# A two-layer DiT block on one core: a fixed order in the V phase of the expert FFN, 1/sqrt on VectorE, and rows held back into the next mixer

## Chip, core and metric

One core of one Trainium2 chip runs the whole kernel in a single launch. The metric is the time of one execution in device microseconds (us). Engines are named as the profile names them: PE (TensorE matmul), PEld (its weight load), DVE (VectorE), ACT (ScalarE), POOL (GpSimd), SP (SyncE, which issues most DMAs).

## The reference, cut to what matters

256 latent tokens (`x`) and 256 context tokens (`ctx`) of width D = 1024 pass through two layers. Layer 0 has an "even" mixer, layer 1 an "odd" one (differential attention; context enters it as keys and values only). Behind each mixer stands a PEER FFN: every token picks 16 of 16384 experts in each of 8 heads. In layer 1 only the latents need the FFN.

```python
def rms_norm(x, g):
    y = x * lax.rsqrt(jnp.mean(x * x, axis=-1, keepdims=True) + EPS)
    return y * g

def modulate(x, g, shift, scale):
    return rms_norm(x, g) * (1 + scale) + shift

def chunk(t):                       # in peer_ffn: 128 tokens
    q = (t @ w_q).reshape(PEER_CHUNK, PEER_HEADS, 2, PEER_KEY_HALF)
    ...
    idx = jnp.take_along_axis(cand_i..., best_j, axis=-1)
    g = jax.nn.softmax(best_s, axis=-1)
    a = jnp.einsum('td,thkd->thk', t, u[idx])
    w = jax.nn.gelu(a) * g
    return jnp.einsum('thk,thkd->td', w, v[idx])

# one layer
hl = modulate(xl, norm_mix_g[layer], sh_m, sc_m)      # and hc from xc
yl, yc = mixer(hl, hc)
xl = xl + g_m * yl
hl = modulate(xl, norm_ffn_g[layer], sh_f, sc_f)
xl = xl + g_f * peer_ffn(hl, w_q, sub_keys, u, v)
# xc likewise in layer 0; six shifts, scales and gates: silu(c) @ w_mod + b_mod
# the end: rms_norm(xl, final_norm_g)
```

## The kernel before

**The FFN, computed densely.** `ffn` (L782) does not gather experts for most tokens. `dense` (L632) runs two phases over all 16384 experts. The U phase computes gelu(h·uT) in 32 chunks of 512 experts. The V phase takes 64 chunks of 256 experts: it multiplies the activations `dy`/`dyl` by the table of gates `dg`, transposes the product on PE and multiplies it by the rows `dv` of V, adding into PSUM (`wide`, `bank`) over all chunks. In layer 0 three blocks of 128 tokens go this way (nt = 3: two of latents, one of context), in layer 1 two (nt = 2). The activations of 16 (layer 0) or 22 (layer 1) of the 64 V chunks stay in SBUF (`dy`); the others go to DRAM (`ad`) and come back as `dyl`.

**Precision.** Each fp32 operand is split in a high part (fp32r, made on ACT: `dvh`, `dwh`, `wh`) and the rest (made on DVE: `dvl`, `dwl`, `wl`), and each product takes three matmuls: high·high (L753), high·low with `dvl` (L754) and low·high (L755).

**One V chunk, as the program is written.** For chunk n: `load_v` (L701) issues from SP `dg` (L706), `dyl` (L710) and two tiles of `dv` (L714, 128 experts each); `v_prep` (L717) makes `dvh` (L724) and `dvl` (L725) of both tiles; `w_prep` (L741) multiplies `dyl` by `dg` (L746) and lets `w_split` (L730) transpose (L733) and split (L737, L738); `v_mm` (L757) multiplies. The loop calls `v_prep(c + 1)`, `load_v(c + 2)`, `w_prep(c + 1)`, `v_mm(c)`. The rings: `dg`, `dyl`, `dv`, `dvh` and `dvl` have 3 buffers, `dwh` and `dwl` 2.

**Who sets the order.** A scheduler with a timeline of its own orders the instructions on each engine when the program is built, so that an engine's order differs from the written one. `tc.issue_after(i)` around an instruction puts it behind `i` on its engine. At run time each engine goes through its list in order: an instruction that waits holds up all behind it.

**The second block of context tokens.** The fourth block of layer 0's FFN goes by row gathers, which run beside the dense phases. `gather` (L547) lets POOL issue an indirect DMA (L549) for one row per token (512 KB, 4 buffers `row`); 256 of them fetch rows of U (dot products on DVE, L564), 128 rows of V, each added on DVE into `gacc` (L576). `beside` (L939) feeds 5, 2 or 3 of these steps per chunk; the odd mixer feeds what is left, 6 per step, then all (L1048). Only when `gacc` is complete is it scaled by a gate and added to `x` (`add_ffn`, L579), and only then can that block be normalised for the odd mixer.

**The end of layer 0 and the odd mixer.** `fin` (L804) makes the gate of the latents' FFN by 8 transposes (L316) and copies (L317), adds the sum of the FFN to `x` (L583 `yadd`, L584 `xl`), and `finish` (L944) calls `norm_T` (L320) for the latents: sum of squares on ACT (L327), 1/sqrt, scaling by DVE (L332 `xn`), transposes on PE (L337), shift and scale (L342, L345 `hf`), split (L348, L349 `h`). The odd mixer projects the latents to q, k and v (weights `wt` split at L187, L188; matmuls L206 to L208; rotation L997 to L1001, with a multiplication on POOL), computes the modulations 3 and 4 of layer 1 (weights `wm`, matmuls L286), and then normalises the context into `oh`, whose tiles are the buffers `row`, and projects it to k and v.

**1/sqrt.** `rsqrt` (L250) starts from an integer estimate on DVE (L253) and makes three Newton steps of 4 operations each on POOL (L255 to L258), for both token blocks together in `norm_T`, where POOL also does the mean (L328), for one block in `rms_scale` (L260), which also makes the final norm's factor.

## Time and profile before

| what | value |
|---|---|
| runs of the kernel | 2888.35, 2892.41, 2897.49 us; median 2892.41 us |
| profiled execution | 2891.71 us, span in the profile 2889.9 us |
| mean granted PE clock of it | 0.965 |
| busy share of the span | PE 90%, PEld 74%, DVE 71%, ACT 45%, POOL 19% |
| data moved by DMA | 735.49 MB, 255 GB/s over the span |

The stages of the profiled execution lie, in us of its span, as follows: layer 0's mixer to about 465, its U phase about 523 to 1098, its V phase 1098 to 1665; the transition to 1697; the odd mixer's projection of latents to 1797, its context and attention to 1912; layer 1's routing and U phase about 2000 to 2438, its V phase 2440 to 2872; the final norm to 2890.

How to read it: a busy share is a mean over these stages. Where an engine waits, the row names the instruction or transfer that ended the wait. The granted clock is a share of full speed.

### The profile page before, as it was taken

The page shows a single profiled execution, that of the slowest core. Times are in us where ns is not written, and L with a number is a line of the kernel's source. Part 1 is how long each engine was busy: PE and PEld are TensorE (multiplying, and loading weights), DVE is VectorE, ACT ScalarE, POOL GpSimd, SP SyncE. Part 2 cuts the span into 40 slices and gives each one's busy share as a digit, 9 for nine tenths or more (in the row PEclk, how much of TensorE's full clock was granted, in tenths as well). Part 3 has the DMA queues.
Part 4 walks back from the last instruction along what each step waited for, and adds up shares of the span by engine and source line. Part 5 has one row for each costly group of instructions (what it writes and reads, how often), then busy time and mean ns, then how long its engine had stood idle before and what let it go on. Part 6 is the DMA issues. An engine that isn't in the chain of part 4 may idle for free.

```text
span 2889.9 us, 40187 instructions
## 1 busy us (share of the span) xinstructions
PE 2610.9 (90%) x14161; PEld 2134.2 (74%) x14161; DVE 2038.6 (71%) x3904; ACT 1310.6 (45%) x2226; POOL 562.0 (19%) x531
## 2 busy tenths in 40 slices
PE   6999984689999989999999969988999999998786
PEld 4776954567777767888888867868888887886665
DVE  3335699999988877887787874766998555554454
ACT  3334432358673433333333334544599743443332
POOL 0000003343433444433344430000000000000000
PEclk9999997899999999999999979999999999999999
DMA  6453466899999999999999856233778975566664
GB/s 246 132 204 86 160 243 206 278 353 345 354 374 354 358 360 351 351 351 351 338 340 358 316 184 231 91 107 127 238 223 266 313 251 180 180 205 214 201 220 140
DMA packets 354634, 735.49 MB, mean 255 GB/s; under 512 B 35312, under 2 KB 182016, under 8 KB 351872
## 3 DMA queue, kind: packets, MB, share of 16 engines
q1 hardware_dynamic: 299136, 531.56, 54.9%
q0 software_dynamic: 55296, 201.35, 19.5%
q8 instruction: 112, 1.84, 0.3%
q14 instruction: 90, 0.74, 0.1%
HBM read 664.13 MB, written 68.68 MB: 254 GB/s over the span
## 4 chain that ended last, share of the span: by engine, by line
PE 50%; issue 16%; DMA 15%; DVE 9%; POOL 6%; ACT 3%; SPq 1%; DVEq 0%; POOLq 0%; ACTq 0%
DMA dyl<-ad 7%; POOL row L549 5%; PE bank L754 4%; PE bank L755 4%; PE bank L207 4%; PE bank L206 4%; PE bank L753 4%; PE bank L208 4%; DMA du<-in_peer_uT 2%; PE bank L671 2%; PE bank L672 2%; PE wide L755 2%; PE wide L754 2%; PE wide L753 2%; PE bank L670 2%
## 5 line engine op out<-in xcount | busy, mean ns | idle before, releaser
L549 POOL DMA_INDIRECT row<-in_peer_u,gidx x256 | 346.7, 1354 | 530.2 <-DVE row L564 423.8
L724 ACT ACTIVATE dvh<-dv 128x1024 fp32r<-128x1024 f32 x256 | 269.4, 1059 | 393.6 <-DMA dv<-in_peer_v 193.6
L657 ACT ACTIVATE duh<-du 128x1024 fp32r<-128x1024 f32 x256 | 271.1, 1062 | 273.3 <-DMA du<-in_peer_uT 217.9
L659 DVE TENSOR_TENSOR dul<-du,duh 128x1024 fp32r<-128x1024 f32 x256 | 310.4, 1218 | 106.6 <-ACT duh L657 105.5
L725 DVE TENSOR_TENSOR dvl<-dv,dvh 128x1024 fp32r<-128x1024 f32 x256 | 309.2, 1222 | 93.0 <-ACT dvh L724 92.9
L564 DVE SCALAR_TENSOR_TENSOR row<-row,hc 128x1024 f32<-128x1024 f32 x256 | 307.3, 1216 | 22.0 <-DMA row<-in_peer_u,gidx 21.6
L754 PE MATMUL bank<-dvl,dwh 128*128 128x512 f32 x768 | 300.9, 392 | 0.5 <-DVE dvl L725 0.5
L755 PE MATMUL bank<-dvh,dwl 128*128 128x512 f32 x768 | 299.8, 392 | 0.0
L188 DVE TENSOR_TENSOR wl<-wt,wh 128x512 fp32r<-128x512 f32 x256 | 177.9, 700 | 157.9 <-ACT wh L187 155.5
L753 PE MATMUL bank<-dvh,dwh 128*128 128x512 f32 x768 | 265.6, 398 | 2.2 <-ACT dvh L724 1.7
L670 PE MATMUL bank<-duh,h 128*128 128x512 f32 x512 | 197.0, 411 | 65.2 <-ACT duh L657 65.1
L187 ACT ACTIVATE wh<-wt 128x512 fp32r<-128x512 f32 x256 | 160.8, 631 | 205.7 <-PE bank L207 98.9
L671 PE MATMUL bank<-dul,h 128*128 128x512 f32 x512 | 213.9, 418 | 11.9 <-DVE dul L659 11.7
L671 PE MATMUL wide<-dul,h 128*128 128x512 f32 x512 | 209.0, 408 | 10.9 <-DVE dul L659 10.9
L549 POOL DMA_INDIRECT row<-in_peer_v,gidx x128 | 170.5, 1332 | 243.7 <-DVE gacc L576 223.7
L670 PE MATMUL wide<-duh,h 128*128 128x512 f32 x512 | 207.0, 404 | 7.5 <-ACT duh L657 7.4
L206 PE MATMUL bank<-h,wh 128*128 128x256 f32 x704 | 206.0, 294 | 5.4 <-ACT hf L342 5.4
L672 PE MATMUL bank<-duh,h 128*128 128x512 f32 x512 | 208.1, 406 | 0.0
L208 PE MATMUL bank<-h,wl 128*128 128x256 f32 x704 | 204.0, 291 | 3.6 <-DVE wl L188 3.6
L207 PE MATMUL bank<-h,wh 128*128 128x256 f32 x704 | 204.5, 291 | 1.1 <-DVE h L349 1.1
L672 PE MATMUL wide<-duh,h 128*128 128x512 f32 x512 | 203.5, 397 | 0.0
L255 POOL TENSOR_TENSOR rs_t<-rstd 128x2 f32<-128x2 f32 (+1 forms) x27 | 7.4, 273 | 936.0 <-DVE rstd L253 934.7
(279 smaller groups left out, 5905.5 us busy)
## 6 DMA issues: line engine op xcount, KB each, us to landing
du<-in_peer_uT SPq DMA_DIRECT2D x256, 512.0 KB, 6.0
dv<-in_peer_v SPq DMA_DIRECT2D x256, 512.0 KB, 5.7
table<-gst SPq DMA_DIRECT2D x80, 512.0 KB, 7.0
wm<-in_w_mod SPq DMA_DIRECT2D x56, 512.0 KB, 6.9
wt<-in_peer_w_q SPq DMA_DIRECT2D x96, 256.0 KB, 3.3
dg<-table SPq DMA_DIRECT2D x64, 384.0 KB, 7.0
ad<-da SPq DMA_DIRECT2D x45, 512.0 KB, 5.4
dyl<-ad SPq DMA_DIRECT2D x90, 256.0 KB, 5.4
```

Of the source, the lines that this page charges most:

```text
L206: self.T.matmul(out, lhsT=a, rhs=b, start=k == 0 and m == 0, stop=False)
L207: self.T.matmul(out, lhsT=a, rhs=b2, start=False, stop=False)
L208: self.last = self.T.matmul(out, lhsT=a2, rhs=b, start=False, stop=k == KT - 1 and m == len(outs) - 1).ins
L549: self.G.indirect_dma_start(out=t, out_offset=None, in_=table, in_offset=bass.IndirectOffsetOnAxis(ap=idx[:, s:s + 1], axis=0))
L659: V.tensor_tensor(tl, t, th.bitcast(F32), ALU.subtract)
L670: T.matmul(b, lhsT=hi[:, k, :], rhs=uh[k], start=k == 0, stop=False)
L671: T.matmul(b, lhsT=hi[:, k, :], rhs=ul[k], start=False, stop=False)
L672: T.matmul(b, lhsT=lo[:, k, :], rhs=uh[k], start=False, stop=k == KT - 1)
L725: V.tensor_tensor(tl, v, th.bitcast(F32), ALU.subtract)
L753: T.matmul(b, lhsT=wh, rhs=v[0], start=first, stop=False)
L754: T.matmul(b, lhsT=wh, rhs=v[1], start=False, stop=False)
L755: T.matmul(b, lhsT=wl, rhs=v[0], start=False, stop=last)
```

## The change

1. **V phase.** For PE, ACT and DVE a helper `placed` puts each step behind the step written before it on the same engine. `v_prep` and `v_mm` are split in halves (one `dv` tile each), the multiplication by `dg` becomes `y_mul`, and the loop is written as shown. `dv` gets 6 - nt buffers: 3 in layer 0 as before, 4 in layer 1.
2. **1/sqrt.** All of it moves to VectorE: per block 3 + 6 small operations. `norm_T` calls it once per block through `rms_scale`.
3. **Gate of the FFN.** It is made when 5 chunks of the V phase are left (`near`), in both layers, into a `dy` buffer.
4. **Rows.** `beside` feeds none in the last two chunks of layer 0's V phase; what is left then is fed in the odd mixer, and put behind the last `xn` of the latents' norm (`normed`).
5. **Modulation 3 of layer 1.** Its first loads begin 8 chunks ahead of the end of layer 0's V phase, its first half is computed with 3 chunks left (`aside`), its second half in `finish`. The odd mixer keeps modulation 4.

```diff
-    def rsqrt(self, y, v, n):
-        G = self.G
-        t = self.small.tile([P, 16], F32, name="rs_t")
-        self.V.tensor_scalar(y.bitcast(I32), v.bitcast(I32), -0.5, 1597463007.0, op0=ALU.mult, op1=ALU.add)
+    def rsqrt(self, y, ss, n, width):
+        V = self.V
+        v, t = (self.small.tile([P, 16], F32, name=f"rs_{x}")[:, :n] for x in "vt")
+        V.tensor_scalar(v, ss, 1.0 / width, EPS, op0=ALU.mult, op1=ALU.add)
+        V.tensor_scalar(y.bitcast(I32), v.bitcast(I32), -0.5, 1597463007.0, op0=ALU.mult, op1=ALU.add)
+        V.tensor_scalar(v, v, -0.5, None, op0=ALU.mult)
         for _ in range(3):
-            G.tensor_tensor(t[:, :n], y, y, ALU.mult)
-            G.tensor_tensor(t[:, :n], t[:, :n], v, ALU.mult)
-            G.tensor_scalar(t[:, :n], t[:, :n], -0.5, 1.5, op0=ALU.mult, op1=ALU.add)
-            G.tensor_tensor(y, t[:, :n], y, ALU.mult)
+            if n == 1:
+                V.scalar_tensor_tensor(t, y, v, y, op0=ALU.mult, op1=ALU.mult)
...
+            V.scalar_tensor_tensor(y, t, 1.5, y, op0=ALU.add, op1=ALU.mult)
...
-        for i in range(2):
-            V.tensor_scalar(xn[i], self.x[2 * s + i], r[:, i:i + 1], None, op0=ALU.mult)
+            r = self.rms_scale(self.x[2 * s + i], xn[i])
+            self.normed = V.tensor_scalar(xn[i], self.x[2 * s + i], r, None, op0=ALU.mult).ins
...
-                    t = vp.tile([P, D], F32, name="dv", bufs=3)
+                    t = vp.tile([P, D], F32, name="dv", bufs=6 - nt)
...
+            def placed(engine):
+                return tc.issue_after(last[engine]) if engine in last else ExitStack()
...
             for c in range(NC):
-                v_prep(c + 1)
+                near(NC - c)
+                y_mul(c + 1)
+                v_prep(c + 1, 0)
                 load_v(c + 2)
+                v_mm(c, 0)
                 w_prep(c + 1)
-                v_mm(c)
+                v_prep(c + 1, 1)
+                v_mm(c, 1)
...
+            def near(n):
+                if n == 5:
+                    gate.append(self.gate(modT, 5, 1, "c", yp, "dy", keep))
+                aside(n, yp, keep)
...
-                feed(5 if c < 26 else 2 if c < NC // 2 else 3)
+                feed(5 if c < 26 else 2 if c < NC // 2 else 3 if c < NC // 2 + NC - 2 else 0)
...
+            if n == 8:
+                mods.append(self.mod_steps(1, 3, mod1, Tags([(yp, "dy", keep)] * 8), "c", keep, Tags([(yp, "dy", keep)] * 2)))
+            if n in (8, 3):
+                next(mods[0])
...
+            def late_rows(n, normed=self.normed):
+                with tc.issue_after(normed):
+                    feed(n)
...
-            if 3 + c < 5:
-                self.modulation(1, 3 + c, modT, wk, "y", 4)
+            if c == 1:
+                self.modulation(1, 4, modT, wk, "y", 4)
```

How the orders move, at the three places of which the prediction speaks. First DVE in the middle of layer 1's V phase; the numbers behind the names are those of tiles, and tiles of one chunk have near numbers (the two `dv` of a chunk stand 2 and 4 above its `dyl`, the next chunk's about 50 higher). Before:

```order
L746 TENSOR_TENSOR dyl_25381<-dyl_25381,dg_25379 128x512
L725 TENSOR_TENSOR dvl_25276<-dv_25235,dvh_25275 128x1024
L725 TENSOR_TENSOR dvl_25322<-dv_25283,dvh_25321 128x1024
L738 TENSOR_TENSOR dwl_25344<-bank_25338,dwh_25343 128x512
L746 TENSOR_TENSOR dyl_25431<-dyl_25431,dg_25429 128x512
L725 TENSOR_TENSOR dvl_25326<-dv_25285,dvh_25325 128x1024
L725 TENSOR_TENSOR dvl_25372<-dv_25333,dvh_25371 128x1024
```

And with the change:

```order
L745 TENSOR_TENSOR dwl_25414<-bank_25408,dwh_25413 128x512
L730 TENSOR_TENSOR dvl_25418<-dv_25344,dvh_25417 128x1024
L752 TENSOR_TENSOR dyl_25390<-dyl_25390,dg_25388 128x512
L730 TENSOR_TENSOR dvl_25448<-dv_25392,dvh_25447 128x1024
L745 TENSOR_TENSOR dwl_25477<-bank_25471,dwh_25476 128x512
L730 TENSOR_TENSOR dvl_25481<-dv_25394,dvh_25480 128x1024
L752 TENSOR_TENSOR dyl_25453<-dyl_25453,dg_25451 128x512
```

Before, the multiplication of a chunk's `dyl` stood ahead of the splits of `dv` that belong to the chunks three and two earlier (`dyl_25431` ahead of `dv_25285` and `dv_25333`); now it stands just ahead of the split of its own chunk (`dyl_25390` ahead of `dv_25392`).

SP in the same phase, before:

```order
L714 DMA dv_24733<-in_peer_v1 128x1024
L710 DMA dyl_24831<-ad1_17939 128x2x256
L714 DMA dv_24735<-in_peer_v1 128x1024
L706 DMA dg_24979<-table1_17938 128x2x256
L714 DMA dv_24783<-in_peer_v1 128x1024
L710 DMA dyl_24881<-ad1_17939 128x2x256
L714 DMA dv_24785<-in_peer_v1 128x1024
L706 DMA dg_25029<-table1_17938 128x2x256
```

And with the change:

```order
L708 DMA dyl_24890<-ad1_18001 128x2x256
L712 DMA dv_24844<-in_peer_v1 128x1024
L704 DMA dg_24938<-table1_18000 128x2x256
L712 DMA dv_24892<-in_peer_v1 128x1024
L708 DMA dyl_24940<-ad1_18001 128x2x256
L712 DMA dv_24894<-in_peer_v1 128x1024
L704 DMA dg_24988<-table1_18000 128x2x256
L712 DMA dv_24942<-in_peer_v1 128x1024
```

Each round still has two `dv`, one `dg` and one `dyl`; before, a `dyl` was asked for between the two `dv` of the chunk two ahead of its own; now between the two `dv` of the chunk just ahead of its own, and `dv` has one buffer more.

Second, DVE at the end of layer 0's V phase, before (the last `dvl`, then the sum of the FFN is added to `x`):

```order
L576 SCALAR_TENSOR_TENSOR gacc<-row,ijgc,gacc 128x1024 x7
L583 TENSOR_TENSOR yadd<-bank,gate 128x512
L576 SCALAR_TENSOR_TENSOR gacc<-row,ijgc,gacc 128x1024
L583 TENSOR_TENSOR yadd<-bank,gate 128x512
L584 TENSOR_TENSOR xl_9947<-xl_9947,yadd 128x512
L576 SCALAR_TENSOR_TENSOR gacc<-row,ijgc,gacc 128x1024
L584 TENSOR_TENSOR xl_9947<-xl_9947,yadd 128x512
L583 TENSOR_TENSOR yadd<-bank,gate 128x512
L576 SCALAR_TENSOR_TENSOR gacc<-row,ijgc,gacc 128x1024
L583 TENSOR_TENSOR yadd<-bank,gate 128x512
L584 TENSOR_TENSOR xl_9949<-xl_9949,yadd 128x512
```

And with the change:

```order
L730 TENSOR_TENSOR dvl<-dv,dvh 128x1024
L581 TENSOR_TENSOR yadd<-bank,gate 128x512 x2
L582 TENSOR_TENSOR xl_9983<-xl_9983,yadd 128x512 x2
L581 TENSOR_TENSOR yadd<-bank,gate 128x512 x2
L582 TENSOR_TENSOR xl_9985<-xl_9985,yadd 128x512
L254 TENSOR_SCALAR rs_v<-ss 128x1
L582 TENSOR_TENSOR xl_9985<-xl_9985,yadd 128x512
L255 TENSOR_SCALAR rstd<-rs_v 128x1
L581 TENSOR_TENSOR yctx<-wide,gate 128x512
L256 TENSOR_SCALAR rs_v<-rs_v 128x1
L581 TENSOR_TENSOR yctx<-wide,gate 128x512
L582 TENSOR_TENSOR xl_9981<-xl_9981,yctx 128x512
```

The rows (`gacc`) that stood between the additions are gone from there; the small operations of the 1/sqrt stand in their place, 18 up to the last `xn`, and no row does. Before, 8 rows stood between the first `yadd` and the last `xn`.

Third, DVE in the odd mixer around the context's norm, before (its `xn` early, among the first splits of weights):

```order
L188 TENSOR_TENSOR wl<-wt,wh 128x512
L332 TENSOR_SCALAR xn<-xl_9943,rstd 128x1024
L332 TENSOR_SCALAR xn<-xl_9945,rstd 128x1024
L188 TENSOR_TENSOR wl<-wt,wh 128x512 x2
L999 TENSOR_TENSOR ru<-bank,c_rope 128x256 x2
L1001 TENSOR_TENSOR oq<-oq,ru 128x256
L188 TENSOR_TENSOR wl<-wt,wh 128x512
L1001 TENSOR_TENSOR oq<-oq,ru 128x256
```

And with the change (the end of the latents' part):

```order
L574 SCALAR_TENSOR_TENSOR gacc<-row,ijgc,gacc 128x1024
L188 TENSOR_TENSOR wl<-wt,wh 128x512
L574 SCALAR_TENSOR_TENSOR gacc<-row,ijgc,gacc 128x1024
L188 TENSOR_TENSOR wl<-wt,wh 128x512
L574 SCALAR_TENSOR_TENSOR gacc<-row,ijgc,gacc 128x1024 x2
L188 TENSOR_TENSOR wl<-wt,wh 128x512 x3
L574 SCALAR_TENSOR_TENSOR gacc<-row,ijgc,gacc 128x1024 x8
L581 TENSOR_TENSOR gacc<-gacc,gate 128x512 x2
L582 TENSOR_TENSOR xl_9979<-xl_9979,gacc 128x512 x2
L254 TENSOR_SCALAR rs_v<-ss 128x1
L255 TENSOR_SCALAR rstd<-rs_v 128x1
```

Before, the context's `xn` came 26 instructions behind the latents' last `xn`, one row among them. Now 56 rows stand between these two, spread over the 48 `wl`, with eight of them last; the gate, the addition to `x`, the 1/sqrt and `xn` come behind those. On POOL 43 gathers stand among the 16 multiplications of the rotation, the last 10 behind all of these.

## Rows read from the trace of the kernel before

**Rows 1.** Windows: stretch, length, busy us (instructions) of each engine, granted clock, DMA share, GB/s.
```profile
1098.00:1666.00 568.00, 562.74 (x2647) 464.70 (x2648) 457.30 (x550) 184.11 (x259) 235.44 (x176) 0.99 0.96 346
1666.00:1697.00 31.00, 4.77 (x21) 3.40 (x19) 27.08 (x41) 7.61 (x17) 12.44 (x20) 0.58 0.46 144
1697.00:1797.00 100.00, 96.48 (x703) 82.72 (x703) 56.42 (x111) 45.44 (x79) 17.73 (x29) 0.98 0.69 237
...
2500.00:2560.00 60.00, 60.00 (x286) 49.63 (x285) 30.52 (x30) 26.88 (x31) 0.00 (x0) 1.00 0.56 177
...
2571.00:2872.00 301.00, 259.46 (x1177) 202.67 (x1176) 144.52 (x161) 106.69 (x123) 0.00 (x0) 1.00 0.64 204
```

**Rows 2.** Waits in 2580:2865: total us, times, longest.
```profile
DVE dyl L746 <- DMA dyl<-ad: 141.8, 37, 5.8
PEld wide L754 <- DVE dvl L725: 56.7, 36, 3.6
```

**Rows 3.** Timeline of layer 1's V phase: start, us, engine, [idle before].
```profile
2643.28 0.69 DVE L746 TENSOR_TENSOR dyl<-dyl,dg 128x512 f32<-128x512 f32 x1 [3.92 <-DMA dyl<-ad]
...
2643.89 2.35 DVE L725 TENSOR_TENSOR dvl<-dv,dvh 128x1024 fp32r<-128x1024 f32 x2
...
2645.16 0.19 PEld L754 LDWEIGHTS wide<-dvl,dwh 128*128 128x128 f32 x1 [1.67 <-DVE dvl L725]
...
2645.55 0.39 SPq L710 DMA_DIRECT2D dyl<-ad  x1
...
2650.66 0.69 DVE L746 TENSOR_TENSOR dyl<-dyl,dg 128x512 f32<-128x512 f32 x1 [3.83 <-DMA dyl<-ad]
```

**Rows 4.** Timeline behind layer 1's V phase: gate, addition, 1/sqrt, last scaling.
```profile
2872.05 1.09 ACT L317 ACTIVATE gate<-bank 128x512 f32<-128x512 f32 x2 [7.59 <-PE bank L316]
2872.68 1.29 DVE L583 TENSOR_TENSOR yadd<-wide,gate 128x512 f32<-128x512 f32 x2 [6.96 <-ACT gate L317]
...
2877.77 0.19 POOL L255 TENSOR_TENSOR rs_t<-rstd 128x1 f32<-128x1 f32 x1 [929.23 <-DVE rstd L253]
...
2879.09 0.15 DVE L253 TENSOR_SCALAR rstd<-ms 128x1 int32<-128x1 int32 x1
...
2883.63 1.28 DVE L965 SCALAR_TENSOR_TENSOR fy<-xl,rstd,fg 128x1024 f32<-128x1024 f32 x1 [1.18 <-POOL rstd L258]
```

**Rows 5.** Timeline from the end of layer 0's V phase to the latents' first projection.
```profile
1657.10 1.86 POOL L549 DMA_INDIRECT row<-in_peer_v,gidx  x1 [1.78 <-DVE gacc L576]
...
1665.20 0.91 PEld L316 LDWEIGHTS bank<-c_ident,modT 128*128 128x128 f32 x7
...
1680.34 0.96 POOL L549 DMA_INDIRECT row<-in_peer_v,gidx  x1 [0.50 <-DVE yctx L583]
...
1682.07 1.16 POOL L255 TENSOR_TENSOR rs_t<-rstd 128x2 f32<-128x2 f32 x1 [0.77 <-DVE rstd L253]
...
1686.10 0.20 POOL L255 TENSOR_TENSOR rs_t<-rstd 128x2 f32<-128x2 f32 x1
...
1688.27 1.42 DVE L332 TENSOR_SCALAR xn<-xl,rstd 128x1024 f32<-128x1024 f32 x2 [2.57 <-POOL rstd L258]
...
1697.09 0.58 PE L207 MATMUL bank<-h,wh 128*128 128x256 f32 x1 [1.07 <-DVE h L349]
```

**Rows 6.** Timeline: the context's first projection.
```profile
1797.13 0.39 PE L206 MATMUL bank<-oh,wh 128*128 128x256 f32 x1 [1.54 <-ACT hf L342]
```

**Rows 7.** Groups by line, DVE in 1666:1797, then PE in 1697:1797: busy us, mean ns.
```profile
L188 DVE TENSOR_TENSOR wl<-wt,wh 128x512 fp32r<-128x512 f32 x48 | 36.0, 759 | 32.1 <-ACT wh L187 30.9 <-PE bank L997 0.9
L576 DVE SCALAR_TENSOR_TENSOR gacc<-row,ijgc,gacc 128x1024 f32<-128x1024 f32 x11 | 14.0, 1276 | 2.6 <-DMA row<-in_peer_v,gidx 2.6
...
L286 PE MATMUL bank<-wm,silu 128*32 128x512 f32 x64 | 13.3, 602 | 0.0
```

**Rows 8.** The page's group of V rows' gathers: busy us, mean ns, idle before.
```profile
L549 POOL DMA_INDIRECT row<-in_peer_v,gidx x128 | 170.5, 1332 | 243.7 <-DVE gacc L576 223.7
```

More of the change, by code (lines that the diff above doesn't have):

```diff
@@ L262, in rms_scale @@
         self.S.activation(scr, xi, AF.Square, accum_out=ss)
-        v = self.small.tile([P, 1], F32, name="ms")
-        self.V.tensor_scalar(v, ss, 1.0 / D, EPS, op0=ALU.mult, op1=ALU.add)
         r = self.small.tile([P, 1], F32, name="rstd")
-        self.rsqrt(r, v, 1)
+        self.rsqrt(r, ss, 1, D)
         return r
@@ L630, in gate_table, with dense @@
             nc.sync.dma_start(table[t0:t0 + 8].rearrange("t (i j) -> i t j", i=P), st)
-    def dense(self, l, tables, hs, ups, yp, keep, mid, late, fin, ad, beside):
-        nc, V, S, G, T = self.nc, self.V, self.S, self.G, self.T
+    def dense(self, l, tables, hs, ups, yp, keep, mid, late, fin, ad, beside, near):
+        nc, tc, V, S, G, T = self.nc, self.tc, self.V, self.S, self.G, self.T
         U = self.A[f"peer_uT{l}"]
@@ L712, in load_v, with v_prep @@
                 for a in range(2):
[L713 removed]
+                    t = vp.tile([P, D], F32, name="dv", bufs=6 - nt)
                     nc.sync.dma_start(t, Vt[2 * c + a])
                     ldv[n].append(t)
[L717 removed]
+            last = {}
+            def placed(engine):
+                return tc.issue_after(last[engine]) if engine in last else ExitStack()
+            def v_prep(n, a):
                 if n >= NC:
                     return
[L720 to L728 removed]
+                th = vp.tile([P, D], F32R, name="dvh", bufs=3)
+                tl = vp.tile([P, D], F32R, name="dvl", bufs=3)
+                v = ldv[n][a]
+                with placed("S"):
+                    last["S"] = S.activation(th, v, AF.Copy).ins
+                with placed("V"):
+                    last["V"] = V.tensor_tensor(tl, v, th.bitcast(F32), ALU.subtract).ins
+                vs.setdefault(n, []).append((th, tl))
             def w_split(name, src, m):
@@ L732, in w_split @@
                 for a in range(m):
-                    T.transpose(b[:, a * P:(a + 1) * P], src(a), self.ident)
+                    with placed("T"):
+                        t = T.transpose(b[:, a * P:(a + 1) * P], src(a), self.ident)
+                last["T"] = t.ins
                 wh = vp.tile([P, m, P], F32R, name=name + "h", bufs=2)
@@ L780, in dense, with ffn @@
             fin(pacc, vp)
-    def ffn(self, l, modT, h, wp, wclose, keep, nt=2, late=iter(()), finish=None, beside=lambda c: None):
+    def ffn(self, l, modT, h, wp, wclose, keep, nt=2, late=iter(()), finish=None, beside=lambda c: None,
+            aside=lambda n, yp, keep: None):
         self.tables = tables = self.dr.tile([nt, P, P * P], F32, name=f"table{l}")
@@ L812, in fin @@
                     finish(pacc[4:])
-            self.dense(l, tables, dense, ExitStack(), yp, keep, mid, late, fin, ad, beside)
+            gate = []
+            self.dense(l, tables, dense, ExitStack(), yp, keep, mid, late, fin, ad, beside, near)
     def run(self):
@@ L1061, in odd_mixer @@
                         head(h, qt, av[:, n:n + P])
-        V.tensor_scalar(ss, ss, 1.0 / P, EPS, op0=ALU.mult, op1=ALU.add)
         r = wk.tile([P, 16], F32, name="orr")
-        self.rsqrt(r, ss, 16)
+        self.rsqrt(r, ss, 16, P)
         for qt in range(2):
```

70 lines of the change are left out of this document (35 added, 35 removed).

## Prediction

> **What bounds the kernel now.** I went by stages, since the shares of the page are means over unlike ones. The windows by stage [rows 1] say in which stages PE has anything to give back. Layer 0's V phase has little: PE is busy for 562.74 of 568 us there, the DMAs for 0.96 of the time and DVE for 457 us. Layer 1's V phase has two halves. While its activations come from SBUF (2500 to 2560) PE is busy throughout; from 2571, when they come back from DRAM, it is busy for 259 of 301 us at the same granted clock of 1.00. The transition behind layer 0 leaves PE 26 of 31 us idle. The latents' part of the odd mixer is PE's again: 96 of 100 us, with DVE busy for 56.4.
>
> The waits of the late V phase [rows 2] name the cause: 36 times PE's weight load waits for a `dvl`, while DVE itself waits 37 times for a `dyl`. The timeline [rows 3] shows how the two hang together. At 2643.28 DVE multiplies a `dyl` after 3.92 us of waiting for it. The two `dvl` that PE needs stand behind it on DVE's list and come at 2643.89; PE has waited 1.67 us when they are done. Only behind them does SP get to the next `dyl`, at 2645.55, and that is multiplied at 2650.66, 5.11 us after its issue. So each chunk asks for its transfer too late and then waits for it: a closed loop of 7.38 us (2643.28 to 2650.66).
>
> **Part 1, layer 1's V phase.** An undisturbed chunk has 28 PE instructions, 60.00/286 x 28 = 5.87 us [rows 1]. The loop's excess is 7.38 - 5.87 = 1.51 us per chunk, 54 us over the 36 waits; the windows say the same: 301 us less 1177 x 60.00/286 = 247 us, 54; the waits' own sum is 56.7 [rows 2]. With the change the `dyl` product no longer stands ahead of older `dvl`; it is held up by its own chunk alone, and SP issues the `dyl` between the two `dv` of the chunk before, with a fourth `dv` buffer. A `dv` buffer comes free when the tile four back is split, two chunks earlier, so the `dyl` is asked for about two chunks (11.7 us) ahead of use and lands in 5.1. DVE's own work per chunk is 0.69 + 2.35 + 0.68, about 3.7 of 5.87 us; the DMAs would move 204 x 7.17/5.87 = 249 GB/s (301 us for 42 chunks is 7.17), and move 346 in layer 0. I take **-55**, bounds -45 (a remnant of 0.3 us per chunk) and -57.
>
> **Part 2, the end of the kernel.** Today the gate's copy starts at 2872.05 and the addition at 2872.68, the last scaling at 2883.63 [rows 4]. With the gate made earlier the addition can start as the last banks close, about 1.2 us sooner. The last 1/sqrt took POOL from 2877.77, for both blocks in turn, to the scaling at 2883.63; on DVE nine operations of 0.15 us are 1.4 us behind the second block's sum of squares. Together **-3.5** (-2 to -5).
>
> **Part 3, 1/sqrt elsewhere.** Other norms ahead of a mixer or an FFN have PE waiting behind them in the same way. The POOL operations take 0.20 us alone but 1.16 beside a row's addition [rows 5]; DVE's small ones 0.15 [rows 4]. Half a microsecond to one for each of four: **-2** (-4 to +1, as they now queue among DVE's rows).
>
> **Part 4, work put into layer 0's V phase.** PE is full there, so it comes on top: the gate's transposes, 0.9 us [rows 5], and half of modulation 3. The four halves of modulations 3 and 4 took 13.3 us [rows 7], so 3.3, and some 0.6 for its transposes. **+5** (+2 to +6). The odd mixer's PE list loses 7.8 us, but see part 5 for who bounds it. The fixed order there gains or loses nothing I can see: DVE keeps about a fifth of slack. Bounds -3 (PE's idle 5 us) to +5.
>
> **Part 5, transition and rows.** V ends at 1665.4; PE restarts at 1697.09, 31.7 later, and the context's first projection at 1797.13, 131.7 later [rows 5, 6]. Without rows between them the twelve additions take 12 x 0.6 = 7.2 us, the 18 small operations 2.7; the latents' `xn` would be done about 10 us behind V's end instead of 24. That frees 14 us of PE idle. But 56 rows now follow, all of which must be in `gacc` before the context can be normalised, and the context's tiles use the rows' buffers. Three things pace them:
> - DVE: 56 x 1.276 [rows 7] = 71 us, beside the 56 us that it had in the odd mixer [rows 1] and 7 for the latents' `hf` and `h`: 124 to 135 us, the lower where operations follow closely (0.6 us per `wl` instead of 0.76 [rows 7]).
> - DMA: 56 rows of 0.524 MB less four already under way, 48 weights of 0.262 and a modulation's 4.2 are 44 MB; at the 346 GB/s of the V phase [rows 1] 127 us.
> - The chain of gather and addition: the 12 gathers from 1657.10 to 1680.34 [rows 5] came 2.11 us apart at a DMA share well under 1; at 0.96 in the V phase 176 came in 568 us [rows 1], 3.2 apart, though there the program itself asked for no more.
>
> I take 2.4 us per row, a little above each of the first two bounds (2.2 to 2.4), since three chains that are nearly full don't mesh perfectly: 134 us. With 10 ahead and 8 for gate, addition, 1/sqrt, transposes and split, the context starts 152 us behind V's end, not 131.7: **+20**. So what the transition gives back is lost again and more: the rows held back become the bound of the odd mixer, and PE's saved modulation is worth nothing. Ends: 2.2 us per row gives +10, 3.2 gives +65.
>
> One rule speaks against holding rows back. The row: a POOL operation of 0.20 us took 1.16 beside a row's addition [rows 5], and a gather 1.33 on average [rows 8], 0.96 in the last of them [rows 5]. The Trainium skill, "SBUF — State Buffer", "SBUF: two separate sides", says that VectorE work on the shared port pair locks GpSimd out, so that it can't write the descriptors of its DMAs meanwhile. The trace agrees as far as the POOL operations go; the gathers it delays by 0.4 us on average, not by a whole addition each. If each waited for a whole one, the sum would be that of the second rival below.
>
> **Sum** against the profiled execution's 2891.71: -55 - 3.5 - 2 + 5 + 20 = -35.5, so 2856. It lies 0.7 below the median of the runs, 2892.41; I say **2857**.
>
> **Rivals.**
> - *The rows mesh as well as they can*: DVE runs through at 2.2 us per row. Then 2891.7 - 57 - 3.5 - 3 + 5 + 10 = **2843**. For: in the rows of the transition DVE hardly idled. Chance 0.15.
> - *POOL is locked out ahead of each gather*: 1.33 + 1.28 = 2.6 us per row and the last eight alone; the start goes to 10 + 56 x 2.7 + 8 = 169, +37, the sum to **2873**. For: the 1.16 against 0.20. Against: the 2.11 us cadence among rows that DVE added without pause. Chance 0.14.
> - *The other side: the rows keep the V phase's pace*, 3.2 us [rows 1], because weights share the queues: +65, **2902**, slower. It decides from 3.0 us per row on, where the loss (18 + 168 - 131.7 = 54, and 5 for part 4) eats all the rest. Against it: in the V phase 3 rows per chunk of 8.8 us were all that was asked for. Chance 0.06.
> - *The change does not do what it says in layer 1*: the `dyl` still comes late, because SP holds it behind a `dv` that waits for its buffer. Then part 1 is gone: 2857 + 55 = **2912**. For: SP is a list too. Against: the two chunks of lead. It decides if a `dyl` is issued less than 5.1 us ahead of use. Chance 0.04.
> - *Layer 0's V phase stalls under the fixed order* with three `dv` buffers and the DMAs at 0.96: 0.6 us in each of 48 loaded chunks, +29, **2886**. Against: the same list of transfers kept PE busy before. Chance 0.04.
>
> **How the numbers follow.** The forecast keeps 0.57. Its own range from the ends of its parts is 2845 to 2872; with the two rivals beside it, 2838 to 2882 leaves out the last three (0.14) and tails of the others. A change of 0.3% (8.7 us) is about what can be told from none: faster means below 2883.7. Forecast and first two rivals are faster, 0.86; the layer 0 stalls are the same, 0.04; the other two are slower, 0.10.
>
> **What would show it.** In layer 1 the wait of `dyl` should be gone from DVE, and PE busy throughout at 5.87 us per chunk, the V phase about 377 us long instead of 432. Behind layer 0's V phase PE should restart about 17 us after its end, with no row among the additions. In the odd mixer DVE should be nearly full, PE should wait for `gacc`-delayed `wl` and at last for the context's `oh`, with the rows 2.2 to 2.6 us apart. I am wrong if the context starts sooner than 140 or later than 165 us behind V's end, or if `dyl` still ends waits.

## The result, and the profile after

The changed kernel takes 2859.76 us (median of 4 runs, 2857.07 to 2861.99), the kernel before 2893.09 us beside it; the ratio is 0.9885, with a 95% interval from 0.9867 to 0.9903. The forecast was 2857. Where the time went is another matter, and the trace shows that two of the forecast's terms were far off and made up for each other. The profiled execution has a span of 2855.3 us, 34.6 less than before.

| stage, bounded by PE instructions | before, us | after, us | difference |
|---|---|---|---|
| start to layer 0's V phase | 1098.2 | 1081.4 | -16.8 |
| layer 0's V phase, first to last product with `dxh` | 566.5 | 572.2 | +5.7 |
| from there to the context's first projection | 132.4 | 171.6 | +39.2 |
| from there to layer 1's V phase | 642.8 | 637.4 | -5.4 |
| layer 1's V phase, first to last product of `wide` with `dwh` | 430.3 | 377.6 | -52.7 |
| from there to the end of the span | 19.7 | 15.1 | -4.6 |

Layer 1's late V phase is what was forecast. In the timeline of one chunk (start, us, engine, idle before) the product with `dyl` waits for nothing, the next comes 5.91 us later, and SP asks for a `dyl` right behind a `dv`; compare the 7.38 us of [rows 3]. In the median a `dyl` is now asked for 14.6 us ahead of its product and lands in 4.1; in the kernel before both took about 5.1, so that the product waited for its transfer:

```profile
2699.53 0.69 DVE L752 TENSOR_TENSOR dyl<-dyl,dg 128x512 f32<-128x512 f32 x1
...
2700.65 1.23 DVE L730 TENSOR_TENSOR dvl<-dv,dvh 128x1024 fp32r<-128x1024 f32 x1 [0.44 <-ACT dvh L728]
...
2702.71 0.38 SPq L708 DMA_DIRECT2D dyl<-ad  x1
...
2705.44 0.69 DVE L752 TENSOR_TENSOR dyl<-dyl,dg 128x512 f32<-128x512 f32 x1
```

The waits of 2595 to 2840 (total us, times, longest) are now all ACT's and DVE's, none of them PE's, and no `dyl` is among them, where [rows 2] had 37 and 36:

```profile
ACT dwh L743 <- PE bank L737: 85.1, 41, 2.1
DVE dwl L745 <- ACT dwh L743: 61.2, 41, 2.4
ACT dvh L728 <- PE bank L773: 48.4, 40, 1.2
```

The windows of the changed kernel (as [rows 1]) show the end of layer 0's V phase, and then layer 1's late V phase with PE busy for 249.91 of 250 us:

```profile
1580.00:1651.00 71.00, 71.00 (x348) 57.74 (x347) 28.44 (x37) 21.86 (x31) 0.00 (x0) 1.00 0.49 156
...
2592.00:2842.00 250.00, 249.91 (x1185) 206.76 (x1183) 155.62 (x167) 108.00 (x125) 0.00 (x0) 1.00 0.77 248
```

The first of the two is a finding: in the last 71 us of layer 0's V phase no row is added (POOL 0.00), DVE is busy for 28 us and the DMAs for half the time. The gap is longer than that: the last addition of a row starts at 1511.5 and the next at 1662.0, so the rows ended some 140 us ahead of the phase's end, although only the last two chunks were to get none. Over that gap DVE is idle for 76 us, room for the 56 additions of 1.28 us that were held back:

```profile
1515.00:1651.00 136.00, 136.00 (x655) 111.80 (x655) 59.63 (x75) 43.42 (x62) 0.00 (x0) 1.00 0.58 185
```

Behind that phase the timeline has no row among the additions, and the 1/sqrt is done 8.9 us after the first addition (in [rows 5] rows came between, and `xn` at 1688.27, 23 us behind the V phase's end). PE restarts at 1667.80, 14 us behind the V phase's end as the table bounds it. Before, that was 31 us: the projection's first matmul stood at 1695.45, and the 1697.09 of [rows 5], which the prediction takes for the restart, is its second:

```profile
1651.05 1.37 DVE L581 TENSOR_TENSOR yadd<-bank,gate 128x512 f32<-128x512 f32 x2 [6.01 <-PE bank L773]
...
1659.99 0.75 DVE L330 TENSOR_SCALAR xn<-xl,rstd 128x1024 f32<-128x1024 f32 x1
...
1661.96 1.28 DVE L574 SCALAR_TENSOR_TENSOR gacc<-row,ijgc,gacc 128x1024 f32<-128x1024 f32 x1
...
1667.80 0.58 PE L206 MATMUL bank<-h,wh 128*128 128x256 f32 x1 [0.84 <-ACT hf L340]
```

The kernel before:

```profile
1695.45 0.57 PE L206 MATMUL bank<-h,wh 128*128 128x256 f32 x1
1697.09 0.58 PE L207 MATMUL bank<-h,wh 128*128 128x256 f32 x1 [1.07 <-DVE h L349]
```

What the held rows cost stands in the next three windows: the transition, PE's projection of the latents, and what then comes before the context's first projection.

```profile
1654.00:1668.00 14.00, 7.58 (x39) 3.91 (x37) 13.86 (x42) 5.41 (x13) 1.69 (x2) 0.73 0.13 37
1668.00:1793.00 125.00, 99.63 (x647) 88.63 (x648) 101.87 (x136) 38.00 (x66) 69.25 (x61) 0.87 0.91 324
1793.00:1825.00 32.00, 4.90 (x19) 3.06 (x17) 24.32 (x47) 7.18 (x14) 8.75 (x7) 0.55 0.50 177
```

The same three of the kernel before:

```profile
1665.00:1695.00 30.00, 4.75 (x24) 3.58 (x23) 26.08 (x37) 5.65 (x12) 12.44 (x20) 0.60 0.50 159
1695.00:1791.00 96.00, 94.93 (x692) 81.78 (x691) 53.58 (x103) 43.64 (x75) 17.73 (x29) 0.96 0.70 239
1791.00:1797.00 6.00, 2.57 (x18) 1.62 (x16) 4.84 (x12) 3.80 (x9) 0.00 (x0) 1.00 0.34 116
```

The transition gives back 16 us. The projection takes 29 us more, although modulation 3 is no longer in it; the DMAs are busy for 0.91 of it, and DVE, at 102 of 125 us, is not full. Then PE stands for another 26 us while the last rows are added and the context is normalised. Its waits from 1662 to 1812 tell how the projection is held up:

```profile
POOL row L547 <- DVE gacc L574: 200.4, 36, 148.7
ACT wh L187 <- DMA wt<-in_odd_w_in: 42.6, 23, 6.8
DVE gacc L574 <- DMA row<-in_peer_v,gidx: 13.0, 10, 2.6
```

ACT waits 42.6 us for the weights `wt`. POOL's total is mostly one wait of 148.7 us that began in the V phase, when the rows stopped; the other 35 are 52 us. PE itself waits for what ACT and DVE make of these weights, 9.2 us for `wh` and 9.4 for `wl` in the same view. The landing times of `wt` (min, median, max), before and after, say the same:

```profile
DMA to landing us min/median/max: 2.9/3.4/7.4
```
```profile
DMA to landing us min/median/max: 3.0/6.3/13.6
```

The held rows' instructions from 1655 to 1830 (duration min, median, max in ns, first and last start):

```profile
L574 DVE SCALAR_TENSOR_TENSOR gacc<-row,ijgc,gacc x56: 1269/1278/2471, 1662.0 to 1811.0; 128x1024 f32<-128x1024 f32 x56
L547 POOL DMA_INDIRECT row<-in_peer_v,gidx x52: 936/1144/1933, 1663.5 to 1805.5; - x52
```

That is a row every 2.7 us (149 us for 55 steps). At the end the last scaling now starts at 2850.47, 10.3 us behind the last product of `wide` with `dwh` at 2840.2; in [rows 4] it was 2883.63, 13.4 behind 2870.2:

```profile
2848.37 1.28 DVE L1007 SCALAR_TENSOR_TENSOR fy<-xl,rstd,fg 128x1024 f32<-128x1024 f32 x1 [0.17 <-DMA fg<-in_final_norm_g]
...
2850.47 1.28 DVE L1007 SCALAR_TENSOR_TENSOR fy<-xl,rstd,fg 128x1024 f32<-128x1024 f32 x1
```

### The profile page after: what moved, and what is told of

The parts are those of the page before. It is cut to its first block, busy times and chain, and to the rows that moved or that the text cites. A ratio compares the mean times of both kernels' runs of the same rounds, so it can differ in the third digit from the quotient of the medians.

```text
span 2855.3 us, 40252 instructions
## 1 busy us (share of the span) xinstructions
PE 2615.0 (92%) x14161; PEld 2152.2 (75%) x14161; DVE 2064.1 (72%) x4047; ACT 1312.5 (46%) x2226; POOL 537.8 (19%) x404
## 3 DMA queue, kind: packets, MB, share of 16 engines
q0 software_dynamic: 55296, 201.35, 19.7%
## 4 chain that ended last, share of the span: by engine, by line
PE 65%; DVE 10%; DMA 10%; issue 8%; POOL 4%; ACT 3%; SPq 0%; POOLq 0%; DVEq 0%; ACTq 0%
PE bank L771 6%; PE bank L773 6%; PE bank L772 6%; PE wide L773 4%; PE wide L771 4%; PE wide L772 4%; POOL row L547 3%; PE bank L206 3%; PE bank L208 3%; PE bank L207 3%; PE bank L626 2%; PE bank L669 2%; PE bank L670 2%; PE bank L668 2%; PE wide L669 2%
## 5 line engine op out<-in xcount | busy, mean ns | idle before, releaser
L547 POOL DMA_INDIRECT row<-in_peer_u,gidx x256 | 344.4, 1345 | 914.7 <-DVE rv L458 429.4
L771 PE MATMUL bank<-dvh,dwh 128*128 128x512 f32 x768 | 289.4, 398 | 0.0
L772 PE MATMUL bank<-dvl,dwh 128*128 128x512 f32 x768 | 283.7, 390 | 0.0
L773 PE MATMUL bank<-dvh,dwl 128*128 128x512 f32 x768 | 263.3, 391 | 0.0
L745 DVE TENSOR_TENSOR dwl<-bank,dwh 128x512 fp32r<-128x512 f32 x128 | 88.5, 691 | 211.1 <-ACT dwh L743 211.1
L743 ACT ACTIVATE dwh<-bank 128x512 fp32r<-128x512 f32 x128 | 76.5, 598 | 327.6 <-PE bank L737 327.5
L206 PE MATMUL bank<-h,wh 128*128 128x256 f32 x704 | 208.1, 296 | 13.5 <-ACT wh L187 5.7
```

The costliest lines, as they stand in the source:

```text
L206: self.T.matmul(out, lhsT=a, rhs=b, start=k == 0 and m == 0, stop=False)
L547: self.G.indirect_dma_start(out=t, out_offset=None, in_=table, in_offset=bass.IndirectOffsetOnAxis(ap=idx[:, s:s + 1], axis=0))
L771: T.matmul(b, lhsT=wh, rhs=vh, start=c == 0 and a == 0, stop=False)
L772: T.matmul(b, lhsT=wh, rhs=vl, start=False, stop=False)
L773: t = T.matmul(b, lhsT=wl, rhs=vh, start=False, stop=c == NC - 1 and a == 1)
```

## The experiments

All ratios are to the kernel before, run beside them. PE's projection of the latents is measured from its first to its last matmul: 95.4 us before (1695.5 to 1790.9), 125.3 with the change (1667.8 to 1793.1).

**One part of the change alone, and two together.** `e_order` is the kernel before with part 1, `e_rsqrt` with part 2, `e_order_rsqrt` with both. Of part 1 only the loop is shown here; `placed`, the halves and the `dv` buffers are those of the change:

```diff
...
-                v_prep(c + 1)
+                y_mul(c + 1)
+                v_prep(c + 1, 0)
                 load_v(c + 2)
+                v_mm(c, 0)
                 w_prep(c + 1)
-                v_mm(c)
+                v_prep(c + 1, 1)
+                v_mm(c, 1)
...
```

> The kernel before with part 1 alone: the fixed order per engine in the V phase, y_mul split off, dv with 6 - nt buffers; 1/sqrt, gate, rows and modulation as before. My theory: the whole gain of layer 1's V phase is in it (432.0 us before, 379.1 with the whole change, so -53) and nothing of the loss in the odd mixer: ratio about 2840/2893 = 0.982, faster than the whole change. Layer 1's V phase 379 +- 3 us, the context's first projection 132 +- 8 us behind the end of layer 0's V phase. Rival: the early gate or the VectorE 1/sqrt is needed for it; then the V phase of layer 1 stays above 400 us and the time above 2865. Second rival: the fixed order costs in layer 0's V phase, which shows in its length (568 us before), and eats more than 10 us.

Measured: 2837.24 us, ratio 0.9803 (0.9775 to 0.983). Layer 1's V phase (first to last product of `wide` with `dwh`) takes 377.9 us, 430.3 before; layer 0's 565.1 (566.5 before), the way from there to the context 135.5. Part 1 holds the whole gain of layer 1's V phase, costs nothing in layer 0, and alone is 22 us faster than the whole change.

> The kernel before with part 2 alone: 1/sqrt on VectorE. With the whole change the work up to the U phase of layer 0 came out 14 us earlier, layer 1 ahead of its V phase 5 us shorter and the end 4.4 us shorter, against the 2 and 3.5 that I gave for all of these. Theory: all three come from the 1/sqrt, so this kernel gains 14 + 5 + 2 and some 2 to 5 in the transition: about 2868. Rival: the 14 us up to the U phase are a new order of the scheduler that any edit could bring; then the gain is 4 to 9 us, about 2885, and PE's first U matmul of layer 0 stays within 4 us of the kernel before.

Measured: 2874.17 us, ratio 0.994 (0.992 to 0.996). PE's first U matmul comes at 510.8 us, 524.9 before. The diff is that of part 2 above. The time lies between the 2868 of my theory and the 2885 of the rival. The 1/sqrt is worth 19 us (12 to 23 by the interval), where parts 2 and 3 of the forecast had 5.5 together for it and the early gate. Its profiled execution took 2884.96 us, 11 above its median, so of its later stages only the short end of the kernel is compared below.

> The kernel before with parts 1 and 2 alone: the fixed order in the V phase and 1/sqrt on VectorE; gate, rows and modulation as before. Alone they took 56 and 19 us off (2837 and 2874 against 2893). Theory: they act in different stages and add up: 2893 - 56 - 19 = about 2818, as much as the change without its held back rows (2817), so that parts 3 and 5 are worth nothing together. Rival: parts 3 and 5 carry 10 us or more of that; then this kernel is at 2827 or above.

Measured: 2816.35 us, ratio 0.9733 (0.9708 to 0.9759). The two parts add up, 56 + 19 = 75 of 75, and with nothing else the kernel is 43 us faster than with the whole change.

**Why layer 1's V phase runs free.** The change has both another order and a fourth `dv` buffer; `e_dv3` is the change without the buffer, `e_dv4` the kernel before with it. The diff is that of `e_dv3`; `e_dv4` has the reverse:

```diff
-                    t = vp.tile([P, D], F32, name="dv", bufs=6 - nt)
+                    t = vp.tile([P, D], F32, name="dv", bufs=3)
```

> The whole change with 3 buffers of dv in layer 1 as before, instead of 4. Theory: what freed layer 1's V phase is the order on DVE (the product with dyl no longer ahead of the splits of older chunks); then the phase stays at 378 to 385 us and the time within 8 us of 2860. Rival: it is the fourth buffer, which lets SP ask for dyl earlier; then the phase is 400 us or longer and the time above 2880.

> The kernel before with a fourth dv buffer in layer 1 and nothing else. Theory (the order decides): the closed loop of dyl's product, two splits and the next issue stays, layer 1's V phase 425 to 435 us and the time 2885 to 2895. Rival (the buffer decides): the phase falls to 379 to 390 us, the time to 2850 or below.

Measured: `e_dv3` 2863.66 us, ratio 0.9924 (0.9899 to 0.9948), layer 1's V phase 377.5 us; `e_dv4` 2891.4 us, ratio 1.0008 (0.9993 to 1.0023), the phase 429.4 us. The order decides, and the buffer is worth nothing that shows. The phase's first and last start in `e_dv3`, then in `e_dv4`, and the wait for `dyl` that `e_dv4` still has between 2600 and 2840:

```profile
L771 PE MATMUL wide<-dvh,dwh x256: 389/389/504, 2464.4 to 2841.9; 128*128 128x512 f32 x128
```
```profile
L753 PE MATMUL wide<-dvh,dwh x256: 387/389/776, 2446.6 to 2876.0; 128*128 128x512 f32 x128
DVE dyl L746 <- DMA dyl<-ad: 123.4, 32, 5.2
```

A `dyl` is asked for 14.6 us ahead of its product in `e_dv3` as in the change, 5.1 ahead in `e_dv4`. The new order is fixed on PE, ACT and DVE at once; that it is DVE's that matters is read from the loop of [rows 3], not tried apart.

**The rows held back.** `e_free_rows` takes part 4 out (three steps in every chunk, and no `issue_after(normed)`). `e_rows35` and `e_rows36` feed more rows in layer 0's V phase, so that 25 and 18 are held back instead of 56; the diff is that of `e_rows35`, the other has `3 + (c % 5 > 1)`:

```diff
-                feed(5 if c < 26 else 2 if c < NC // 2 else 3 if c < NC // 2 + NC - 2 else 0)
+                feed(5 if c < 26 else 2 if c < NC // 2 else 3 + c % 2 if c < NC // 2 + NC - 2 else 0)
```

> The whole change without part 4: three row steps per chunk to the end of layer 0's V phase, and what is left not put behind the latents' norm. Theory: the held back rows cost the 39 us by which the odd mixer's latents came out longer (171.0 us from the end of layer 0's V phase to the context's first projection, 131.7 before); without them this stretch is at most 132 us and the time about 2821 (39 less than 2860), while the transition itself is longer again than the 9 us of the change. Rival: the stretch is bound by its weights and PE's order and stays above 150 us, the time above 2845.

> The whole change, but three and four row steps in turn per chunk of layer 0's V phase instead of three, so that 25 rows are held back behind the latents' norm and not 56. In the change's trace DVE is busy for 28 of the last 71 us of that phase and the DMAs for 0.49, with no row among them. Theory: 31 rows of 1.28 us fit there at no cost, and 25 rows leave DVE about 40 us less in the odd mixer, so that PE sets its pace again: context's first projection 110 to 120 us behind the V phase's end (171 now), time about 2860 - 55 = 2805. Rival: with more rows layer 0's V phase stalls on its transfers (DMA share 0.93 to 0.96 there), which gives back 20 us or more: above 2825.

> The whole change with 3.6 row steps per chunk of layer 0's V phase, so that 18 rows are held back and not 56 (25 with 3.5 steps: 2816.9), with no row among the additions behind that phase. Theory: every held row costs the odd mixer its bytes. PE's projection of the latents there took 125 us with 56 rows, 107 with 25, 95 in the kernel before, so some 0.57 us per row; 7 rows fewer give 4 us: about 2813, projection 103 us. Rival: the projection's length is set by something else (order of the weights, PE's clock) and stays at 107 or more; the time at 2817 or above.

| kernel | rows held | time, us (ratio) | transition | projection | rest to the context | layer 0's V phase |
|---|---|---|---|---|---|---|
| the change | 56 | 2859.76 (0.9885) | 14 | 125 | 32 | 572.2 |
| `e_rows35` | 25 | 2816.88 (0.974, 0.9714 to 0.9765) | 14 | 108 | 6 | 570.3 |
| `e_rows36` | 18 | 2816.39 (0.9739, 0.9719 to 0.9759) | 16 | 101 | 6 | 575.7 |
| `e_free_rows` | none | 2817.11 (0.9744, 0.9718 to 0.9769) | 33 | 86 | 6 | 575.5 |

Part 4 costs 43 us. It is not the holding back as such, but its amount: with 18 or 25 rows the short transition is kept, yet each row then takes its share in the projection, so the sum is the same as without any (16 + 101 + 6 = 123 against 33 + 86 + 6 = 125). My 2805 for `e_rows35` was too low by 12, since I thought that PE would set the pace there. For `e_rows36` I had said 2813: the projection got 7 us shorter, as expected, but layer 0's V phase 5 us and the transition 2 us longer. Windows of `e_rows36` (V phase's end, transition, projection) and of `e_free_rows` (transition, projection):

```profile
1580.00:1661.00 81.00, 79.94 (x384) 63.13 (x382) 54.67 (x63) 23.98 (x34) 29.60 (x20) 1.00 0.80 294
1661.00:1677.00 16.00, 7.99 (x34) 4.08 (x32) 15.22 (x43) 6.09 (x13) 1.97 (x2) 0.66 0.12 33
1677.00:1778.00 101.00, 91.53 (x652) 83.15 (x651) 72.16 (x133) 41.70 (x72) 30.48 (x29) 0.92 0.74 255
```
```profile
1657.00:1690.00 33.00, 7.84 (x36) 4.45 (x34) 30.91 (x61) 6.38 (x13) 10.70 (x9) 0.60 0.50 158
1690.00:1776.00 86.00, 85.40 (x649) 78.59 (x650) 52.00 (x112) 41.53 (x71) 12.91 (x16) 0.97 0.65 220
```

**What paces the held rows, DVE or the DMAs.** `e_half_add` halves DVE's work on a V row (the other half of that sum is left out). `e_half_row` halves the bytes of the 56 rows and leaves DVE's work as it is (each half row is added twice, so the sum is another one). The second diff is cut:

```diff
-                V.scalar_tensor_tensor(acc, t, a[:, s:s + 1], acc, op0=ALU.mult, op1=ALU.add)
+                V.scalar_tensor_tensor(acc[:, :512], t[:, :512], a[:, s:s + 1], acc[:, :512], op0=ALU.mult, op1=ALU.add)
```
```diff
+    def gather_half(self, gp, table, idx, s):
...
+        self.G.indirect_dma_start(out=t[:, :512], out_offset=None, in_=table.rearrange("e (h d) -> (e h) d", h=2),
...
+            if s >= 72:
+                t = self.gather_half(gp, self.A[f"peer_v{l}"], idx, s)
+                a2 = acc.rearrange("p (h d) -> p h d", h=2)
+                V.scalar_tensor_tensor(a2, t, a[:, s:s + 1], a2, op0=ALU.mult, op1=ALU.add)
...
```

> The whole change, but each of the 127 additions of a V row takes 512 of its 1024 columns (the other half of that sum is left out); the gathers still fetch whole rows. It halves DVE's work on the 56 held back rows, 56 x 0.6 = 33 us, and leaves the DMAs alone. From the end of layer 0's V phase to the context's first projection the change takes 171.6 us, the kernel before 132.4. Theory A (DVE's list paces the rows there): about 140 us. Theory B (the DMAs pace them: 0.92 busy in that stretch, weights landing in 6.3 us instead of 3.4): 160 us or more.

> The whole change, but the last 56 row gathers fetch 512 elements per token (rows of a halved view of V) and DVE adds each half twice, so that DVE's work stays and the bytes fall by 56 x 0.262 = 14.7 MB, 45 us at the 327 GB/s of that stretch; that part of the sum is another one than the reference's. Theory A (DVE): the 171.6 us stay above 160. Theory B (DMA): 125 to 140 us. If each of the two halvings takes off something, the two chains hinder each other.

Measured, one execution each: `e_half_add` 2851.71 us, 164.3 us from the V phase's end to the context (1652.8 to 1817.1); `e_half_row` 2846.44 us, 160.6 (1651.3 to 1811.9). By their words the first fits theory B (160 or more) and the second theory A (above 160); each takes something off the 171.6, 7 and 11 us. The whole way thus doesn't decide, and the windows have to. Projection of `e_half_add`:

```profile
1667.00:1793.00 126.00, 99.75 (x648) 86.25 (x648) 80.72 (x139) 38.42 (x66) 66.38 (x64) 0.91 0.92 334
```

Projection and rest of `e_half_row`:

```profile
1665.00:1763.00 98.00, 87.69 (x646) 78.94 (x647) 85.30 (x122) 39.16 (x68) 59.50 (x49) 0.97 0.80 268
1763.00:1812.00 49.00, 4.99 (x21) 3.24 (x20) 41.24 (x62) 7.53 (x15) 23.84 (x19) 0.53 0.46 134
```

With DVE at 81 us instead of 102 the projection is as long as in the change, 126 us; with half the bytes it falls to 98. The weights' landing times (min, median, max) in `e_half_add` and in `e_half_row`:

```profile
DMA to landing us min/median/max: 3.0/6.9/14.5
```
```profile
DMA to landing us min/median/max: 3.5/4.5/11.3
```

The kernel to compare with is `e_free_rows`, which has the same projection without modulation 3 and no row in it: 86 us (the 95 of before hold modulation 3 as well). So of the 39 us by which the change's projection is longer, 27 go with half the rows' bytes and 12 stay. In `e_half_row` also fewer additions start within the projection, 32 instead of 44. That this is not what shortens it, `e_rows35` says: 22 whole rows there and 108 us, more than with 32 half rows. So it is mainly the rows' bytes, landing among the weights, that hold PE's projection up. Not all of the 39 us is waiting: with nearly the same list of matmuls PE was busy for 85.4 us in `e_free_rows` and 99.6 in the change, 14 us more, at a granted clock of 0.97 and 0.87.

The rest, from the projection's end to the context, is another matter. It falls from 32 to 24 us in `e_half_add`, and in `e_half_row` it grows to 49: there the scheduler put 19 additions behind the last split of a weight (8 in the change), and those now stand alone. That it is the order that holds the rows up there, and not their transfer, is likely for the change's own rest as well, since POOL's gathers wait for `gacc` 36 times and DVE's additions for a row 10 times. How long the rest would be with half the bytes and the change's own order was not tried.

**Parts 3 and 5 of the change (early gate, modulation 3).** `e_free_nomod` is the change without parts 4 and 5:

> The change without parts 4 and 5: rows not held back, modulation 3 of layer 1 back in the odd mixer. Theory: modulation 3 costs layer 0's V phase about as much PE time (4 of its 8 us) as it spares the odd mixer, where PE is again the bound without the held rows, with the other half in PE's idle time: this kernel 2 to 6 us slower than the 2817 of the change without part 4. Rival: modulation 3's weights (4.2 MB) and matmuls in the busy V phase cost more than they spare: equal or faster than 2817.

Measured: 2818.92 us, ratio 0.975 (0.9729 to 0.9771). Against 2817.11 with part 5 that is no difference that can be told, where I had expected 2 to 6 us. Layer 0's V phase is 566.0 us instead of 575.5; the way to the context is longer by 8.5 (133.5 against 125.0). What modulation 3 costs in one place it spares in the other. And as `e_order_rsqrt`, with neither part 3 nor 5, is at 2816.35, the early gate brings nothing that shows either. At the end of the kernel that can be seen directly: from the last product of `wide` with `dwh` to the end it takes 19.7 us before, 18.1 in `e_order`, 16.5 in `e_rsqrt`, and 15.0 in `e_order_rsqrt` as 15.1 in the change. Under the fixed order the scheduler put the gate's copies ahead of that product by itself (2806.0 and 2809.9, the product at 2810.1, in `e_order_rsqrt`).

**Where the 1/sqrt gains.** `e_perblock` calls `rms_scale` for each block in `norm_T`, as the change does, but with POOL's Newton steps:

```diff
...
-        self.G.tensor_scalar(ss, ss, 1.0 / D, EPS, op0=ALU.mult, op1=ALU.add)
-        r = self.small.tile([P, 2], F32, name="rstd")
-        self.rsqrt(r, ss, 2)
         for i in range(2):
-            V.tensor_scalar(xn[i], self.x[2 * s + i], r[:, i:i + 1], None, op0=ALU.mult)
+            r = self.rms_scale(self.x[2 * s + i], xn[i])
+            V.tensor_scalar(xn[i], self.x[2 * s + i], r, None, op0=ALU.mult)
```

> The kernel before, with the latents' and context's norms calling rms_scale once per block of tokens as the change does, but with the Newton steps still on POOL (DVE makes the mean and the first estimate). Part 2 alone brought PE's first U matmul of layer 0 from 524.9 to 510.8 us and the time down by 19 us. Theory: it is the engine that counts, since POOL's steps come late among gathers and DVE's rows; then the first U matmul stays at 520 us or later here and the time at 2885 or above. Rival: handling the blocks apart, with the order that the scheduler finds for it, brings the gain; then the first U matmul is at 515 us or earlier and the time at 2878 or below.

Measured: 2888.8 us, ratio 0.9991 (0.9977 to 1.0005): the split alone brings nothing. What brings the 19 us is the move to VectorE, or the fused operations that came with it (6 instead of 12 for the steps); the two were not separated. PE's first U matmul comes at 515.8 us here, where I had said 520 or later. So the start of the U phase can move by 9 us with the scheduler's order and bring nothing to the end (the context's first projection is at 1795.0, 1797.1 before), and the 14 us at that point in `e_rsqrt` are not to be taken as the gain itself. Nor do they come from a shorter norm. Here is the latents' norm ahead of the U phase and the first U matmul, in the kernel before:

```profile
392.61 1.41 DVE L332 TENSOR_SCALAR xn<-x,rstd 128x1024 f32<-128x1024 f32 x2
...
524.94 1.22 PE L670 MATMUL bank<-duh,h 128*128 128x512 f32 x2 [50.68 <-ACT duh L657]
```

And in `e_rsqrt`:

```profile
399.81 0.74 DVE L330 TENSOR_SCALAR xn<-x,rstd 128x1024 f32<-128x1024 f32 x1
...
510.81 1.22 PE L668 MATMUL bank<-duh,h 128*128 128x512 f32 x2 [22.83 <-ACT duh L655]
```

There the small operations stand among others on DVE's list and take from 378.8 to 399.6, where the 1/sqrt with POOL's steps took from 385.5 to 389.4; `xn` comes 7 us later, and the U phase starts earlier all the same. Which order of which engine brings that was not taken apart.

**A better version.** `e_order_rsqrt`, `e_rows36`, `e_rows35` and `e_free_rows` lie within 1 us of each other, at 2816 to 2817: 43 us below the change and 76 below the kernel before.

## Why the prediction was right, and where it was not

The parts here are those of the prediction, not those of the change.

- **Part 1, layer 1's V phase: right.** -55 forecast, -52.7 measured, by the mechanism given: `e_order` has the gain with this part alone, and `e_dv3` and `e_dv4` leave the order as its cause. A chunk takes 5.91 us (5.87 forecast), the DMAs move 248 GB/s (249), and a `dyl` is asked for 14.6 us ahead of use (11.7 forecast). One reason given with it falls: the fourth buffer.
- **Part 2, the end: right.** -3.5 forecast, -4.6 measured, and the same without the early gate (`e_order_rsqrt`): the fixed order alone brings 1.6 of it and the 1/sqrt 3.2.
- **Part 3, 1/sqrt elsewhere: wrong.** -2 forecast with -4 as its end; alone the 1/sqrt is worth 19 us, about 16 without the end of the kernel. The step that failed is "half a microsecond to one for each of four": I priced each norm by the difference of the operations' durations. In the norm ahead of layer 0's U phase the 1/sqrt takes 20.8 us on DVE where it took 3.9, and the U phase still starts 14 us earlier, so the gain there is not that of a shorter norm. `e_perblock` shows that it isn't the split by blocks either; where it comes from stays open.
- **Part 4, work in layer 0's V phase: right in its sum.** +5 forecast, +5.7 measured. It is made up otherwise: the fixed order gave 1.4 back (`e_order` 565.1, 566.5 before), the gate cost 0.9 (`e_free_nomod` 566.0), and the half of modulation 3 about 6 in the change and 9.5 in `e_free_rows`, not 3.9.
- **Part 5, transition and rows: right in its sign, wrong in size.** +20 forecast, +39.2 measured, and the context starts 171.6 us behind V's end, beyond the 165 that I had named as the bound of being right. The transition gives back 16 us (14 forecast). The rows come 149 us from first to last start, 2.7 us apart, not 2.4, and the step that failed is the 2.4 us itself, taken as a little above DVE's and the DMAs' own bounds. `e_half_add` and `e_half_row` show what was missing: the rows' bytes delay the weights, and so PE. The DMAs moved 324 GB/s there, not the 346 that I took. That late weights then hold DVE's splits, and these the additions behind them, is how I read the order; it was not tried apart. Then gate, addition, 1/sqrt, `xn` and split take 13 us (1812.3 to 1825.2), not 8.
- **The rivals.** The pace of the V phase (3.2 us per row) did not come, nor did a late `dyl` or a stall in layer 0's V phase. The lockout of POOL, priced at 2.6 to 2.7 us per row, met the cadence, but not by its mechanism: a gather took 1.14 us in the median with DVE busy for 102 of 125 us, as over all 128 gathers of V rows before (median 1.14, mean 1.33 [rows 8]), POOL waited for `gacc` to free a buffer, and halving DVE's additions left the projection as long as it was. The rule behind it, from the Trainium skill, "SBUF — State Buffer", "SBUF: two separate sides", says that GpSimd can't write descriptors while VectorE runs an operation in a 2-port perf mode; the prediction left that condition out. No run here shows the rule at work on the gathers.
- **The sum** came out at 2856 for 2857.07 of the profiled execution because the two misses, about +19 in part 5 and about -20 in part 3 and what it moves (the stages ahead of layer 0's and layer 1's V phase, -22.2 together), cancel. That the number is right is luck.

## What to carry to other kernels

Where an engine waits for a transfer whose issue stands behind work that the same engine still has to do, the cure was here the order, not another buffer: move the consumer of the transfer behind the work that others wait for. Work that is deferred must be counted in bytes in the stage that it is moved to, against the loads that this stage can't go without; look first whether the stage that it leaves has idle time at its end. And try the parts of a change one by one: here two of five carry all of the gain, and one takes more than half of it back.
